# First stage of a hybrid decoder step: the first pair of sequences compressed one at a time, and GpSimd asking for the loads that are not pages

## The chip, the cores and the metric

The kernel runs on one core of a Trainium2 chip. The metric is device time in microseconds (us) for one execution; the median of several runs is given, and the profile is of one more execution. Engines are called as in the profile: PE (TensorE), PEld (its weight loads), DVE (VectorE), ACT (ScalarE), POOL (GpSimd) and SP (SyncE). SPq, ACTq and POOLq are the instruction streams of SP, ACT and POOL in so far as they issue DMAs. All arithmetic inputs and outputs are float32.

## The reference, cut to what matters

One inference step of a one-layer decoder: 512 prompt tokens and 8 sequences of 8 new tokens each, width 1024. Each of the 8 sequences has 2048 past tokens in a paged cache of 128-token pages, 16 pages each, found through `page_table`. The part that the change touches is the compression of the raw keys and values of the past (`compress_blocks`), the norm and the adaLN modulation ahead of the input projection:

```python
def compress_blocks(x, pos, w1, w2):          # x: (sequence, 2048 tokens, 2 groups, 64)
    xc = x.reshape(b, 128, 16, 2, 64)          # chunks of 16 tokens
    lead  = einsum('bncgd,cdh->bngh', xc + pos[0], w1[0])
    trail = einsum('bncgd,cdh->bngh', xc + pos[1], w1[1])
    return einsum('bngh,hd->bngd', silu(lead[:, :-1] + trail[:, 1:]), w2)
# kc = rms_norm(compress_blocks(k_raw, ...)), vc = compress_blocks(v_raw, ...)
mod = silu(c) @ w_ada + b_ada                  # shift, scale, gate
h = rms_norm(x, norm1_g) * (1 + sc1) + sh1
z = h @ w_in                                   # then attention, mixing and the MLP
```

## The kernel before, in words

The first stage (`first_stage`) compresses the past of the 8 sequences, and beside it norms and turns x and computes the first eight pieces of the modulation. The projection `z`, attention and the MLP follow it.

**Units.** The stage is a row of 32 units. Unit `u` works on a pair of sequences `i = u // 8`, on one of four groups of taps `j = (u // 2) % 4`, and on keys or values `kv = u % 2`. For each, DVE copies the page tile `cpg` of each sequence into order (`cmp_order`, tile `ro`, one for two units), PE turns it (`rows_turn`, PSUM tile `ct`, four transposes for each sequence), ACT rounds it into `xh` and DVE takes the rest into `xl` (`split`), in a ring of two buffers. Then PE makes twelve products `hid` over the 512 columns of the pair (`cmp_hidden`). High and low parts of values and weights are kept apart so that three fast products stand for one exact one. In the first eight units the weights of the taps are split in the same way (`cmp_taps`, tiles `w1hlk`, `w1hlv` from `w1rawk`, `w1rawv`).

**Order.** PE's matmuls of this stage are chained in the order of the program text: the turns of unit `u + 1` stand ahead of the products of unit `u`. What else is to be done is hung behind units in the list `todo`: the silu of c (`ada_silu`), the turned constants, the bias of the compression (`posb`), the norm of an x tile (`norm`: a Square on ACT, a short chain on DVE) and its turn one unit later (`nt`), the sums of `w_ada` pieces (`ada`), and the ends of each pair (`cmp_act`, `cmp_out`, `cmp_keys`). For ACT and DVE a planner orders the instructions by a time line of its own, except where the text puts one behind another (`issue_after`).

**Queues.** `dma` puts each transfer behind the previous one of the same engine, so SP's list is in the order of the text. It holds the page table, nearly all pages (each an instruction of 128 KB, its number read from the table into a register; eight numbers are read at once), the x tiles, c, the small constants, `w2` and the `w_ada` pieces. ACT's list holds the first tap weights, eight pages of sequence 1, and the other tap weights. GpSimd issues only two gathers here. The page tile `cpg` has four buffers, the x tile two, and the two raw tap weights share their two buffers (`big`) with the `w_ada` pieces.

Of the kernel before, what the change touches and what calls it, by code (L numbers as in the profile page):

```python
# [45 lines left out]
class Step:  # L46
# [165 lines left out]
    def constants(self):  # L212
        nc, I, c = self.nc, self.I, self.const_tile
        gains = c("gains", [8, P])
        pos = c("pos", [32, P])
        chan = c("chan", [64, P])
        for i, n in enumerate("kv"):
            self.dma("sync", pos[16 * i:16 * i + 16], I[f"cmp_pos_{n}"].rearrange("o (j c) d -> (o j) (c d)", c=2))
        self.dma("sync", c("ptT", [P, 1], I32), I["page_table"].rearrange("b (n o) -> (b n) o", o=1))
        self.dma("sync", chan[0:48], I["b_ada"].rearrange("o (j p) -> (o j) p", p=P))  # L220
        self.dma("sync", chan[48:56], I["norm1_g"].rearrange("o (j p) -> (o j) p", p=P))
        self.dma("sync", chan[56:64], I["norm2_g"].rearrange("o (j p) -> (o j) p", p=P))
        for i, n in enumerate(["fox_qn_g", "nsa_qn_g", "nsa_kn_cmp_g"]):
            self.dma("sync", gains[i:i + 1].rearrange("o (a d) -> o a d", a=2),
                                dram(I[n], 0, [[64, 1], [0, 2], [1, 64]]))
# [13 lines left out]
    def late_constants(self):  # L239
# [13 lines left out]
        kgain = c("kgain", [P, 3, 64])  # L253
        for i, n in enumerate(["fox_kn_g", "nsa_kn_slc_g", "nsa_kn_win_g"]):
            self.dma("sync", kgain[:, i, :], dram(I[n], 0, [[0, P], [1, 64]]))
        self.dma("sync", c("bfox", [P, 8]), dram(I["b_fox_f"], 0, [[0, P], [1, 8]]))
        ts(c("identB", [P, P], BF16), jp, 0.0, None, OP.is_equal)
        ts(c("diagB", [P, P], BF16), jp, 0.0, NEG, OP.is_gt, OP.mult)
        ts(c("triU", [P, P]), jp, 0.0, None, OP.is_ge)


    def ada_start(self):
# [3 lines left out]
        self.dma("sync", c9[0:1], self.I["c_prompt"].rearrange("o (k c) -> o k c", k=NK))  # L266
        self.dma("sync", c9[1:9], self.I["c_sample"].rearrange("b (k c) -> b k c", k=NK))
        self.c9 = c9, c9t
# [17 lines left out]
    def ada_load(self, ch, w):  # L286
        self.dma("sync", w, self.I["w_ada"][0, :, 256 * ch:256 * ch + 256].rearrange("(k p) e -> p k e", p=P))
# [63 lines left out]
    def cmp_weights(self, pl):  # L351
# [7 lines left out]
        for i in range(2):  # L359
            x = [pl.tile([P, 2, 514], F32R, name=f"x{n}{i}") for n in "hl"]  # L360
            for t in x:
                self.nc.vector.memset(t[:, :, 512:514].bitcast(F32), 0.0)
            self.ring.append(x)

    def cmp_taps(self, u):

        taps = lambda w: w.rearrange("p (a j) h -> p a j h", a=4)[:, :, u // 2]
        w = self.w1[u % 2]
        self.split(taps(w[:, 0]), taps(w[:, 1]), taps(self.w1raw[u % 2]))

    def cmp_second(self):

        self.w2 = []
        for n in "kv":
            w2 = self.keep.tile([P, 64], F32, name=f"w2{n}")
            w2r = self.keep.tile([P, 64], F32, name=f"w2raw{n}")
            self.dma("sync", w2r, self.I[f"cmp_w2_{n}"][0])
            self.ts(w2, w2r, 0.5, None, OP.mult)
            self.w2.append(w2)
# [57 lines left out]
    def cmp_order(self, pl, n):  # L437

        self.ros[n] = []
        for b in (2 * (n // 4), 2 * (n // 4) + 1):  # L440
            o = pl.tile([P, 2, 4, 2, 64], F32, tag="ro", bufs=3, name=f"ro{n}_{b}")
            self.cp(o.rearrange("p h x c d -> p h c x d"),
                    self.cpg[b][:, :, 2 * (n % 4):2 * (n % 4) + 2].rearrange("p h c (x d) -> p h c x d", x=4))
            self.ros[n].append(o)

    def rows_turn(self, u):


        n, kv = u // 2, u % 2
        xh, xl = self.ring[u % 2]  # L450
        for s in range(2):
            tb = self.trb(f"ct{u}{s}")
            for g in range(2):
                for h in range(2):
                    self.tr(tb[:, 256 * g + P * h:256 * g + P * h + P],
                            self.ros[n][s][:, h, 2 * kv + g].rearrange("p c d -> p (c d)"))
# [5 lines left out]
    def cmp_hidden(self, u):  # L462
        i, j, kv = u // 8, (u // 2) % 4, u % 2
        if u % 8 == 0:
# [34 lines left out]
    def first_stage(self, pl, pe, hf):  # L499
# [21 lines left out]
        def late():  # L521
            with self.tc.issue_after(self.splits[-1]):
                self.late_constants()
# [20 lines left out]
        todo = {u: [] for u in range(32)}  # L544
        todo[4] += [self.ada_silu]
        todo[5] += [self.constants_turned, self.ada_turned, lambda: ends.update(b=self.cmp_bias(pe)),
                    lambda: self.ada_first_load(pe, 4), lambda: self.ada_first_load(pe, 0)]
        todo[6] += [lambda: self.cmp_bias_end(ends["b"])]
        todo[8] += [late]
# [3 lines left out]
        for b, u in ((4, 4), (5, 6), (6, 12), (7, 14)):  # L553
            todo[u] += [load_x] * (b < 6) + [lambda b=b: self.cmp_tile(pe, b), lambda b=b: self.cmp_pages("sync", b)]
        todo[10] += [load_x]
        for k, u in enumerate((9, 11, 17, 19, 21, 23, 25, 27)):
            todo[u] += [lambda k=k: ends.update({k: self.ada_first(pe, ada[k])})]
            todo[u + 1] += [lambda k=k: ends[k]()]
            if k > 1:
                todo[(12, 14, 18, 20, 22, 24)[k - 2]] += [lambda k=k: self.ada_first_load(pe, ada[k])]  # L560
            if k % 2:
                todo[max(u + 2, 17)] += [lambda k=k: self.modulate(0, hf, range(k - 1, k + 1))]
        self.lfg = {}
        for y, u in enumerate((15, 18)):
            todo[u] += [lambda y=y: self.stage_logf(pe, y)]
            todo[u + 2] += [lambda y=y: self.store_logf(y)]
        for i in range(3):
            for kv in range(2):
                todo[8 * i + 6 + kv] += [lambda i=i, kv=kv: self.cmp_act(pl, i, kv)]
        for i in range(3):  # L570
            for kv in range(2):
                todo[8 * i + 10 + kv] += [lambda i=i, kv=kv: self.cmp_out(pl, i, kv)]
            todo[8 * i + 13] += [lambda i=i: self.cmp_keys(i)]
# [3 lines left out]
        for u in range(32):  # L577
            if u % 2 == 0 and u // 2 + 1 < 16:
                self.cmp_order(pl, u // 2 + 1)
            if u + 1 < 8:  # L580
                self.cmp_taps(u + 1)
            if u + 1 < 32:
                self.rows_turn(u + 1)
            self.cmp_hidden(u)
# [1561 lines left out]
```

## Time and profile before

| | |
|---|---|
| runs | 1265.33, 1269.34, 1272.30 us; median 1269.34 us |
| profiled execution | 1271.95 us, span 1270.1 us |
| busy in the span | PE 1196.8, PEld 1022.9, DVE 695.5, ACT 509.3, POOL 108.9 us |
| matmul clock granted, mean | 0.985 |
| first transposes of pages on PE | at 26.71 us |
| first compression products on PE | at 35.66 us |
| last compression products on PE | end at about 190 us |

In the lines of the timeline a row reads: start in us, time in us, engine, line of the kernel, operation, output and inputs with shapes, count, and in brackets the engine's idle time before it with what ended it. In the chain of waits a row is start, length, and what held the chain. Rows that group instructions give count, busy us, mean ns, and idle time before them. A busy time sums neighbouring, pipelined instructions into their union. In the rows of DMA issues the last number is the median us from issue to landing.

### The profile page before, as it was taken

The page shows a single profiled execution, that of the slowest core. Times are in us where ns is not written, and L with a number is a line of the kernel's source. Part 1 is how long each engine was busy: PE and PEld are TensorE (multiplying, and loading weights), DVE is VectorE, ACT ScalarE, POOL GpSimd, SP SyncE. Part 2 cuts the span into 40 slices and gives each one's busy share as a digit, 9 for nine tenths or more (in the row PEclk, how much of TensorE's full clock was granted, in tenths as well). Part 3 has the DMA queues.
Part 4 walks back from the last instruction along what each step waited for, and adds up shares of the span by engine and source line. Part 5 has one row for each costly group of instructions (what it writes and reads, how often), then busy time and mean ns, then how long its engine had stood idle before and what let it go on. Part 6 is the DMA issues. An engine that isn't in the chain of part 4 may idle for free.

```text
span 1270.1 us, 24582 instructions
## 1 busy us (share of the span) xinstructions
PE 1196.8 (94%) x9379; PEld 1022.9 (81%) x9379; DVE 695.5 (55%) x1888; ACT 509.3 (40%) x1135; POOL 108.9 (9%) x107
## 2 busy tenths in 40 slices
PE   0799999999999999999999998989999999999998
PEld 0677778999666656666799998988989899898896
DVE  2577775676688846555543444666234433333545
ACT  2344444443776854544432323353414123232230
POOL 0000000000221120000200000001011111020110
PEclk9999999999999999999999999998999999999999
DMA  9576518697685359797663233124213223142202
GB/s 205 163 227 188 174 57 271 192 331 230 192 280 177 108 198 302 257 297 245 154 171 92 76 92 100 51 67 133 67 67 100 82 86 100 34 133 67 67 18 75
DMA packets 177067, 188.09 MB, mean 148 GB/s; under 512 B 16901, under 2 KB 158766, under 8 KB 174774
## 3 DMA queue, kind: packets, MB, share of 16 engines
q1 hardware_dynamic: 168134, 178.13, 45.7%
q0 software_dynamic: 3504, 5.24, 1.6%
q10 hardware_dynamic: 5312, 3.15, 1.1%
q8 instruction: 74, 1.21, 0.4%
q14 instruction: 43, 0.35, 0.1%
HBM read 176.48 MB, written 30.90 MB: 163 GB/s over the span
## 4 chain that ended last, share of the span: by engine, by line
PE 84%; DVE 5%; SPq 4%; DMA 4%; ACT 2%; issue 1%; DVEq 0%; ACTq 0%
PE up L77 16%; PE dn L77 16%; PE z L77 8%; PE mg L77 8%; PE wo L77 4%; PE br L77 4%; PE hid L77 4%; PE ss L77 4%; SPq L155 4%; PE k L83 2%; PE so L77 2%; DMA cpg<-in_cache_nsa_kv 2%; PE sp L83 1%; PE ada L77 1%; PE ct L83 1%
## 5 line engine op out<-in xcount | busy, mean ns | idle before, releaser
L77 PE MATMUL z<-winh,h 128*128 128x264 f32 (+1 forms) x576 | 112.2, 287 | 2.4 <-DVE h L723 1.7
L77 PEld LDWEIGHTS z<-winh,h 128*128 128x128 f32 x576 | 92.0, 190 | 5.4 <-DVE h L723 4.2
L1935 POOL TENSOR_TENSOR u<-u 128x576 f32<-128x576 f32 x32 | 53.0, 1659 | 426.8 <-ACT u L112 337.6
L77 PE MATMUL z<-winl,h 128*128 128x264 f32 (+1 forms) x320 | 88.0, 284 | 0.0
L100 DVE TENSOR_TENSOR acc<-acc,dn 128x512 f32<-128x512 f32 x60 | 39.8, 686 | 74.5 <-PE dn L77 74.4
L77 PE MATMUL mg<-hH,wmh 128*128 128x288 f32 x256 | 75.9, 298 | 1.1 <-ACT wmh L112 1.1
L77 PE MATMUL mg<-hH,wml 128*128 128x288 f32 x256 | 75.6, 297 | 0.9 <-DVE wml L131 0.9
L77 PE MATMUL mg<-hL,wmh 128*128 128x288 f32 x256 | 72.7, 295 | 0.0
L83 PE MATMUL ct<-identF,ro 128*128 128x128 f32 x256 | 36.6, 289 | 36.4 <-DVE ro L115 30.3
L112 ACT ACTIVATE xh<-ct 128x256 fp32r<-128x256 f32 x128 | 47.5, 385 | 57.0 <-PE ct L83 35.8
L83 PEld LDWEIGHTS ct<-identF,ro 128*128 128x128 f32 x256 | 30.6, 149 | 40.7 <-DVE ro L115 30.7
L723 DVE TENSOR_TENSOR u<-u,u 128x512 fp32r<-128x512 f32 x64 | 28.3, 484 | 60.8 <-ACT u L112 60.8
L77 PEld LDWEIGHTS z<-winl,h 128*128 128x128 f32 x320 | 60.6, 190 | 0.0
L131 DVE TENSOR_TENSOR xl<-ct,xh 128x256 fp32r<-128x256 f32 x128 | 50.2, 419 | 13.0 <-ACT xh L112 10.2
L131 DVE TENSOR_TENSOR wml<-wmr,wmh 128x1024 fp32r<-128x1024 f32 x16 | 19.6, 1225 | 63.8 <-ACT wmh L112 63.8
L77 PEld LDWEIGHTS mg<-hH,wmh 128*128 128x128 f32 x256 | 48.5, 189 | 1.5 <-ACT wmh L112 1.3
L77 PEld LDWEIGHTS mg<-hH,wml 128*128 128x128 f32 x256 | 48.6, 190 | 1.1 <-DVE wml L131 1.1
L112 ACT ACTIVATE u<-up 128x256 f32<-128x256 f32 (+1 forms) x96 | 27.8, 326 | 52.1 <-PE up L77 51.1
L77 PEld LDWEIGHTS mg<-hL,wmh 128*128 128x128 f32 x256 | 47.1, 188 | 0.1
L77 PE MATMUL hid<-xh,w1hlk 128*128 128x512 f32 x128 | 43.3, 420 | 0.0
L77 PE MATMUL hid<-xh,w1hlv 128*128 128x512 f32 x128 | 41.7, 407 | 0.0
L112 ACT ACTIVATE u<-u 128x576 fp32r<-128x576 f32 x32 | 21.9, 686 | 41.8 <-POOL u L1935 41.8
(928 smaller groups left out, 3553.1 us busy)
## 6 DMA issues: line engine op xcount, KB each, us to landing
adw<-in_w_ada SPq DMA_DIRECT2D x16, 1024.0 KB
foxD<-in_cache_fox_kv SPq DMA_DIRECT2D x128, 128.0 KB
wur<-in_w_up SPq DMA_DIRECT2D x32, 512.0 KB
wdr<-in_w_down SPq DMA_DIRECT2D x32, 512.0 KB
cpg<-in_cache_nsa_kv SPq DMA_DIRECT2D x120, 128.0 KB
fr<-foxD SPq DMA_DIRECT2D x28, 512.0 KB
sr<-in_cache_nsa_kv SPq DMA_DIRECT2D x112, 128.0 KB
wada<-in_w_ada SPq DMA_DIRECT2D x8, 1024.0 KB
```

The costliest lines, as they stand in the source:

```text
L77: ins = self.nc.tensor.matmul(out, a, b, start=start, stop=stop, skip_group_check=True)
L83: ins = self.nc.tensor.transpose(out, in_, self.identF[:n, :n])
L100: self.nc.vector.tensor_tensor(out, a, b, op=op)
L112: return self.nc.scalar.activation(out, in_, f, **kw)
L131: self.splits.append((eng or self.nc.vector).tensor_tensor(l, x, h.bitcast(F32), op=OP.subtract).ins)
L155: self.issued[eng] = getattr(self.nc, eng).dma_start(out, in_).ins
L723: (eng or self.nc.vector).tensor_tensor(h2[:, o:o + n], x[:, i:i + n], h2[:, i:i + n].bitcast(F32), op=OP.subtract)
L1935: nc.gpsimd.tensor_tensor(u[j], u[j], u[j], op=OP.mult)
```

## The change

The 32 units become 40. The first pair's two sequences are done one after the other in eight units each, on 256 columns (`units` lists for each unit its pair, its sequences, `j` and `kv`); the other three pairs keep their eight units of 512 columns. The ring's zero columns are set behind each half. The taps are split in the first eight units as before, now pinned behind the previous unit's last `xh` and `xl`, as are the `ro` copies up to unit 15 and each that begins a new sequence or pair.

SP's list in this stage is left with the page table and pages: eight of sequence 0, all of 1, 2, 3, and later 4 to 7 (and the two stores of gathered log forget values, as before). ACT's eight pages are the second half of sequence 0. All else is issued by GpSimd, in the order of its use: c and the small constants at the start, two x tiles when `xl` of the units 4 and 6 is there (a one-element copy on GpSimd makes it wait), `w2`, the page table's second form, the key gains and the forget bias behind unit 10, then x tiles and `w_ada` pieces in turn. A Tanh of one column is run on ACT ahead of its pages. The constants that DVE computes stand at the start, not behind unit 8; the halving of `w2` is done in place behind unit 18. What hangs behind units is moved on by eight (by eight to ten for some).

The diff, cut:

```diff
@@ constants, late_constants, ada_start @@
-            self.dma("sync", pos[16 * i:16 * i + 16], ...)
-        self.dma("sync", c("ptT", [P, 1], I32), ...)
-        self.dma("sync", chan[0:48], ...)
+            self.dma("gpsimd", pos[16 * i:16 * i + 16], ...)
+        self.dma("gpsimd", chan[0:48], ...)
...
+    def late_loads(self):
+        self.dma("gpsimd", c("ptT", [P, 1], I32), ...)
+        kgain = c("kgain", [P, 3, 64])
+        for i, n in enumerate(["fox_kn_g", "nsa_kn_slc_g", "nsa_kn_win_g"]):
+            self.dma("gpsimd", kgain[:, i, :], ...)
+        self.dma("gpsimd", c("bfox", [P, 8]), ...)
...
-        self.dma("sync", c9[0:1], self.I["c_prompt"]...)
-        self.dma("sync", c9[1:9], self.I["c_sample"]...)
+        self.dma("gpsimd", c9[0:1], self.I["c_prompt"]...)
+        self.dma("gpsimd", c9[1:9], self.I["c_sample"]...)
@@ ada_first_load @@
-        self.ada_load(ch, w)
+        self.ada_load(ch, w, "gpsimd")
@@ cmp_order, rows_turn @@
+        _, bs, j, _ = self.units[u]
+        for b in bs:
+            o = pl.tile([P, 2, 4, 2, 64], F32, tag="ro", bufs=3, name=f"ro{b}_{j}")
...
-        for s in range(2):
+        for b in bs:
+            s = b % 2
             tb = self.trb(f"ct{u}{s}")
@@ cmp_hidden @@
+        c0, w = 256 * (bs[0] % 2), 256 * len(bs)
-            for w, x in three((wh, wl), self.ring[u % 2]):
-                self.mm(self.hid[i][kv], w[:, 4 * a + j, :], x[:, a % 2, a // 2:a // 2 + 512], n == 0, n == 47)
+            for y, x in three((wh, wl), self.ring[u % 2]):
+                self.mm(self.hid[i][kv][:, c0:c0 + w], y[:, 4 * a + j, :], x[:, a % 2, c0 + a // 2:c0 + a // 2 + w],
+                        n == 0, n == 47)
@@ first_stage @@
-            self.dma("sync", xs[k][:TILES[k][1]], self.x_rows(k))
+            self.dma("gpsimd", xs[k][:TILES[k][1]], self.x_rows(k))
+        def behind():
+            both = ExitStack()
+            for i in (self.last_high, self.splits[-1]):
+                both.enter_context(self.tc.issue_after(i))
+            return both
+        self.units = [(b // 2, bs, j, kv) for b, bs in ((0, (0,)), (1, (1,)), (2, (2, 3)), (4, (4, 5)), (6, (6, 7)))
+                      for j in range(4) for kv in range(2)]
-        self.cmp_pages("sync", 0)
-        self.cmp_pages("scalar", 1, slice(0, 8))
+        warm = self.small.tile([P, 1], F32, tag="warm", bufs=1, name="warm")
+        nc.vector.memset(warm, 0.0)
+        self.act(warm, warm, AF.Tanh)
+        self.cmp_pages("sync", 0, slice(0, 8))
+        self.cmp_pages("scalar", 0, slice(8, 16))
         self.cmp_raw(pe, 1)
-        self.cmp_pages("sync", 1, slice(8, 16))
+        self.cmp_pages("sync", 1)
         self.cmp_weights(pl)
-        self.cmp_pages("sync", 2)
-        load_x()
-        self.cmp_pages("sync", 3, slice(0, 8))
-        load_x()
         self.ada_start()
         self.constants()
-        self.cmp_pages("sync", 3, slice(8, 16))
-        self.cmp_second()
+        self.late_constants()
+        self.cmp_pages("sync", 2)
+        self.cmp_pages("sync", 3)
-        todo[4] += [self.ada_silu]
+        todo[9] += [pinned(self.ada_silu)]
+        todo[10] += [self.cmp_second, self.late_loads]
+        todo[18] += [pinned(self.cmp_second_half)]
-        for k, u in enumerate((4, 6, 9, 11, 15)):
-            todo[u - 1] += [lambda k=k: norm(k)]
+        for k, u in enumerate((12, 14, 17, 19, 23)):
+            todo[u - 2] += [lambda k=k: norm(k)]
             todo[u] += [lambda k=k: turned(k)]
+        def asked():
+            x = self.ring[0][1]
+            g = nc.gpsimd.tensor_copy(warm, x[:, 0, 0:1].bitcast(F32))
+            with self.tc.issue_after(g.ins):
+                load_x()
+        todo[3] += [asked]
+        todo[5] += [asked]
+        todo[8] += [pages(4)]
+        todo[12] += [load_x]
+        todo[13] += [wada(0)]
+        todo[14] += [pages(5), load_x]
+        todo[15] += [wada(1)]
+        todo[18] += [load_x]
+        todo[20] += [pages(6)]
+        todo[22] += [pages(7)]
-        for k, u in enumerate((9, 11, 17, 19, 21, 23, 25, 27)):
+        for k, u in enumerate((17, 19, 25, 27, 29, 31, 33, 35)):
...
-                todo[(12, 14, 18, 20, 22, 24)[k - 2]] += [lambda k=k: self.ada_first_load(pe, ada[k])]
+                todo[(20, 22, 26, 28, 30, 32)[k - 2]] += [wada(k)]
...
-        for u in range(32):
-            if u % 2 == 0 and u // 2 + 1 < 16:
-                self.cmp_order(pl, u // 2 + 1)
+        for u in range(40):
+            if u % 2 == 0 and u + 2 < 40 and (u + 2) % 8:
+                with behind() if u + 2 < 16 else nullcontext():
+                    self.cmp_order(pl, u + 2)
             if u + 1 < 8:
-                self.cmp_taps(u + 1)
+                with behind():
+                    self.cmp_taps(u + 1)
             self.rows_turn(u + 1)
+            if (u + 2) % 8 == 0 and u + 2 < 40:
+                with behind():
+                    self.cmp_order(pl, u + 2)
             self.cmp_hidden(u)
```

More of the change, by code (lines that the diff above doesn't have):

```diff
@@ L361, in cmp_weights @@
             for t in x:
-                self.nc.vector.memset(t[:, :, 512:514].bitcast(F32), 0.0)
+                for c in (256, 512):
+                    self.nc.vector.memset(t[:, :, c:c + 2].bitcast(F32), 0.0)
             self.ring.append(x)
     def cmp_taps(self, u):
-        taps = lambda w: w.rearrange("p (a j) h -> p a j h", a=4)[:, :, u // 2]
-        w = self.w1[u % 2]
-        self.split(taps(w[:, 0]), taps(w[:, 1]), taps(self.w1raw[u % 2]))
+        _, _, j, kv = self.units[u]
+        taps = lambda w: w.rearrange("p (a j) h -> p a j h", a=4)[:, :, j]
+        w = self.w1[kv]
+        self.split(taps(w[:, 0]), taps(w[:, 1]), taps(self.w1raw[kv]))
     def cmp_second(self):
@@ L519, in turned, with pinned, g @@
                 self.copy(hf[:, 4 * h:4 * h + 4, t0:t0 + m], self.norm_turned(xs[k], 0, k, h))
-        def late():
-            with self.tc.issue_after(self.splits[-1]):
-                self.late_constants()
+        def behind():
[3 more added lines that the diff above has]
+            return both
+        def pinned(f):
+            def g():
+                with behind():
+                    f()
+            return g
+        self.units = [(b // 2, bs, j, kv) for b, bs in ((0, (0,)), (1, (1,)), (2, (2, 3)), (4, (4, 5)), (6, (6, 7)))
+                      for j in range(4) for kv in range(2)]
         self.page_rows()
@@ L548, in first_stage @@
-        todo[6] += [lambda: self.cmp_bias_end(ends["b"])]
-        todo[8] += [late]
-        for k, u in enumerate((4, 6, 9, 11, 15)):
-            todo[u - 1] += [lambda k=k: norm(k)]
-            todo[u] += [lambda k=k: turned(k)]
-        for b, u in ((4, 4), (5, 6), (6, 12), (7, 14)):
-            todo[u] += [load_x] * (b < 6) + [lambda b=b: self.cmp_tile(pe, b), lambda b=b: self.cmp_pages("sync", b)]
-        todo[10] += [load_x]
-        for k, u in enumerate((9, 11, 17, 19, 21, 23, 25, 27)):
+        todo = {u: [] for u in range(40)}
```

75 lines of the change are left out of this document (37 added, 38 removed).

## The prediction

> **What bounds the kernel now.** I read the page first, then busy time by stretch, the chain of waits, and the timelines of the queues and engines. On the page, the chain that ended last:
>
> ```profile
> PE 84%; DVE 5%; SPq 4%; DMA 4%; ACT 2%; issue 1%; DVEq 0%; ACTq 0%
> ```
>
> TensorE sets the end; SP's list and DMA hold 8%, some 100 us. Busy times by stretch (length, then PE, PEld, DVE, ACT, POOL, clock, DMA share, GB/s) say where the rest lies:
>
> ```profile
> 26.70:35.60 8.90, 3.77 (x16) 3.00 (x17) 4.90 (x10) 2.20 (x6) 0.00 (x0) 1.00 0.56 162
> 35.60:50.60 15.00, 15.00 (x73) 12.49 (x73) 6.63 (x15) 4.46 (x12) 0.00 (x0) 1.00 0.70 208
> 50.60:78.60 28.00, 22.11 (x176) 18.29 (x175) 18.08 (x64) 12.17 (x28) 1.21 (x1) 0.94 0.49 144
> 78.60:190.00 111.40, 107.78 (x696) 85.72 (x694) 82.94 (x282) 52.99 (x128) 0.98 (x1) 1.00 0.55 160
> ```
>
> PE begins at 26.7. At 78.6 the eighth unit of the first pair has passed its `hid` products. From there to 190, the rest of the first stage, PE idles 3.6 of 111.4 us. So after 78.6 the stage is PE's own work, and whatever brings 78.6 forward should bring the end forward. Before it PE is idle for 26.7 + 5.1 + 5.9 us. The timelines show on what (PE, then ACT, then SP's list):
>
> ```profile
> 26.71 1.12 PE L83 MATMUL ct<-identF,ro 128*128 128x128 f32 x4 [26.71 <-DVE ro L115]
> ...
> 35.66 1.20 PE L77 MATMUL hid<-xh,w1hlk 128*128 128x512 f32 x2
> ...
> 39.84 1.04 PE L83 MATMUL ct<-identF,ro 128*128 128x128 f32 x8
> ...
> 55.56 1.90 PE L83 MATMUL ct<-identF,ro 128*128 128x128 f32 x8 [4.54 <-DVE xl L131]
> 57.11 1.20 PE L77 MATMUL hid<-xh,w1hlk 128*128 128x512 f32 x2
> ```
> ```profile
> 12.80 1.62 ACTq L155 DMA_DIRECT2D w1rawv<-in_cmp_w_v  x2
> 14.45 1.28 ACT L112 ACT_TABLE_LOAD   x1 [14.45 <-DMA cpg<-in_cache_nsa_kv]
> 15.75 2.19 ACT L112 ACTIVATE w1hlk<-w1rawk 128x512 fp32r<-128x512 f32 x4
> 22.72 2.19 ACT L112 ACTIVATE w1hlv<-w1rawv 128x512 fp32r<-128x512 f32 x4 [4.79 <-DMA w1rawv<-in_cmp_w_v]
> ...
> 52.66 1.05 ACT L112 ACTIVATE adw<-adw 9x1024 f32<-9x1024 f32 x1 [3.77 <-DMA adw<-in_c_sample]
> ```
> ```profile
> 2.92 38.10 SPq L155 DMA_DIRECT2D cpg<-in_cache_nsa_kv  x40
> ...
> 49.56 0.76 SPq L155 DMA_DIRECT2D adw<-in_c_sample  x1
> ```
>
> Two things stand out. The first `hid` waits until 35.66, because a unit needs the pages of both sequences. And at 48.9 ACT, which works in order, stands on the Tanh over c_sample, whose load SP asks for only at 49.56, behind page after page; `xh` stands behind it, PE idles 4.5 us, and starts again slowly (the eight `ct` at 55.56 take 1.90, those at 39.84 1.04).
>
> **The change, part by part.** *When the first half-width units can run.* The order of bytes hardly changes until 14 us: SP still sends eight pages of sequence 0 first, and ACT's eight pages are now the other half of the same sequence instead of half of sequence 1. ACT's queue goes in order, and behind those pages come the two halves of w1rawv, which the split at 22.72 finds landed. So ACT's pages have landed by 22.7 at the latest, SP's first eight well before: sequence 0 is ready at 17 to 22 us, and the first `ct` follows one copy later, against 26.7 now. But the second unit needs the v taps: w1rawv at 22.7, plus the table load that the new warm Tanh puts ahead of ACT's pages, 1.28 us, partly under the wait for the page table (0.4 taken, bounds 0 and 1.28), plus one tap on ACT (2.19/4) and one on DVE, then `xh` and `xl`. Its `hid` starts at 25.0 (bounds 23.5 and 28).
>
> *PE's work from there to the end of the first pair.* From the chain of waits and the groups by shape:
>
> ```profile
> 139.48 2.79 PE hid L77 x12
> ...
> 142.49 0.87 PE ct L83 x8
> ...
> 211.52 12.96 PE z L77 x107
> ```
> ```profile
> L131 DVE TENSOR_TENSOR xl<-ct,xh 128x256 fp32r<-128x256 f32 x128 | 50.2, 419 | 13.0 <-ACT xh L112 10.2
> L131 DVE TENSOR_TENSOR w1hlv<-w1rawv,w1hlv 128x512 fp32r<-128x512 f32 x4 | 2.6, 686 | 4.5 <-ACT w1hlv L112 4.5
> L115 DVE COPY ro<-cpg 128x1024 f32<-128x1024 f32 x32 | 21.1, 690 | 14.6 <-PE ct L83 11.3 <-DMA cpg<-in_cache_nsa_kv 3.1
> ```
>
> A pair's unit costs PE 2.79 + 0.87 = 3.66 us. Half as wide, twelve `hid` products of 256 columns cost 12 × 0.121 (the pace of the 264-wide `z`) = 1.45, and four `ct` 0.44: 1.89 us. Their sum over 16 units is 30.2 against 29.3, so the doubled weight loads cost about 1 us; I use 1.89. After the first unit and the second's `ct`, 30.2 - 1.89 - 0.44 = 27.9 is left. Other work between 50.6 and 78.6 (bias, two x tiles turned): 22.11 - 4 × 3.66 = 7.5, of which the slow restart is about 1.8 (those `ct` hold PE 1.55 until `hid` begins instead of 0.87, and the first two `hid` behind them take 1.20 as at 35.66, where twelve lost 1.4 in all; I take 1.1); 5.7 is left, and the restart goes with the stall, c_sample being asked for in the first microseconds. The cold beginning stays: 4.2 us from 35.66 to 39.84 for one `hid`, 1.4 over the warm 2.79. Idle time is what I know least: the old stretch had 1.35 beside the stall, and half units leave less cover, since two `xh` and two `xl` after a `ct` take about as long as the 1.89 us that PE has meanwhile. I take 5. Sum: 25.0 + 27.9 + 5.7 + 1.4 + 5 = 65.0.
>
> *DVE's work in the same stretch.* 4.90 + 6.63 + 18.08 = 29.6 us, plus seven taps, which used to be done before PE began and now stand pinned between the units: 7 × 0.69 = 4.8. Together 34.4. The most that DVE was busy in a ten-microsecond stretch of the first stage is this:
>
> ```profile
> 80.00:90.00 10.00, 8.07 (x55) 5.88 (x53) 8.34 (x45) 4.32 (x11) 0.00 (x0) 1.00 1.07 323
> ```
>
> At that share, 34.4/0.834 = 41.2, so 66.2. PE's and DVE's ends fall together, and where two bounds are level the result is a little behind both: I take 67.3, 11.3 us before 78.6.
>
> *Pages for the next pair.* Sequences 2 and 3 must be there some 4 us before that. The new list of SP has 24 pages to the end of sequence 1, as the old one had to the middle of sequence 1; these rows of the chain give the next group and its pitch, and a landing:
>
> ```profile
> 28.33 0.53 SPq L162
> ...
> 34.71 0.52 SPq L162
> ...
> 79.89 9.09 DMA x<-in_x_prompt
> ...
> 108.16 2.58 DMA cpg<-in_cache_nsa_kv
> ```
>
> Four groups of eight at 6.4 us end at 53.9, landed at 56.5: no wait. If the two x tiles (1 MB), now in a queue beside, slow SP's pages to the 162 GB/s of 26.7:35.6, it is some 63, level with the need. What comes off SP's list hides nothing after that: the remaining pages have more lead than before.
>
> *Loads by GpSimd.* Its engine is idle all through this stage, and its own rows late in the kernel give the price:
>
> ```profile
> hH<-hfd POOLq DMA_DIRECT2D x1, 2304.0 KB, 13.1
> hL<-hfd POOLq DMA_DIRECT2D x8, 256.0 KB, 4.9
> ```
>
> Interpolated, a 512 KB x tile lands in about 6 us, 1 MB of w_ada in 8. The tight one is the third x: asked for at unit 12, squared on ACT after unit 15, three half units and two turned tiles later, about 8 us. In order behind that Square stand ACT's `xh`, then DVE and PE. At the 9.1 us of the x row above it costs 1 to 2 us; on the other side the constants now run while DVE is idle at the start, and the halving of w2 no longer stands ahead of `xl`. I let the two cancel (bounds -2 and +3). The w_ada loads have two or more full units of lead. GpSimd's new one-element copies wait for `xl`; behind them stand only its own loads, and the `xl` two units later waits for a copy that is long done: 0. The added memsets and the moved constants lie before the first page. After 190 nothing is edited; I shift it whole.
>
> The Trainium skill speaks against this part: "SBUF — State Buffer", section "SBUF: two separate sides", says that a DMA asked for by GpSimd cannot get its descriptors written while a VectorE copy in a two-port mode holds the shared port, and gives 620 ns growing to 3100. No row here shows it. By it each of the three tightly timed x tiles would land up to 2.5 us later, the sum would lose up to 7.5, and the gain would be about 4.
>
> *Sum.* The profiled execution took 1271.95 us with a span of 1270.1 and 1.85 around it; the median of the runs, 1269.34, lies 2.6 lower. 1271.95 - 11.3 = 1260.6 against the profile, 1258.0 as a median. With idle 1.35 and full speed the pair ends near 62 (gain 16); with idle 9, near 71.5 (gain 7): 1253 to 1262.
>
> **The rivals.** *DVE becomes the bound (18%).* For it: 34.4 us of DVE work, now in strict order with the units; its share in 50.6:78.6 is 0.65, in 78.6:190 0.745. Against it: PE, not DVE, set the pace there. At 0.745 the pair ends at 71.2, at 0.65 at 78: gain 7.4 to 0.6, 1262 to 1269.
>
> *GpSimd's loads come late (12%), slower.* Each x holds one of two buffers, so x tiles three, four and five follow one another in one in-order queue with w_ada between, and each late microsecond holds ACT, then PE. The forecast's 11.3 is used up when the five x and first w_ada loads together come 11.3 us late; it is slower by over 0.5% from 17.7 late. With x landing at 14 instead of 8 us three times, and a slow restart of 1.8 each, 23 us are lost: 1281. For it: the load row of 9.1 us. Against it: GpSimd's landings of 4.9 and 13.1 us, on calmer DMA. The rule of the port would push this way, yet not this far.
>
> *The clock stays low (8%), slower.* After an idle stretch PE runs at about half speed: 1.20 for two `hid` and 1.90 for eight `ct`. If the gaps between half units never let it warm, each costs up to 1.89 us more, sixteen some 29 over the 1.4 counted, less the 5 of idle time that this fills: 1282 if all are cold, 1270 if half. It decides from about ten units. Against it: at the old start one group of twelve was enough (the `ct` at 39.84 are quick), and a PE that is slow has no gaps. The Trainium skill, "TensorE: Matmul & The Clock Gate", section "Part 1: The HAM clock gate", has it cool only after an idle window of about 3.4 us; the trace agrees in so far as the 4.54 us at 55.56 did it. By that rule gaps of well under a microsecond leave it warm.
>
> *The change doesn't do what it says (2%)*: the planner lets another wait stand where c_sample's stood; 1269.
>
> **How the numbers follow.** A measurement tells 0.5%, 6.3 us, from no change: below 1263 is faster. Forecast 60%, all faster. DVE 18%, half faster, half the same. Loads 12% and clock 8%, slower. Nothing done 2%, the same. So 0.69, 0.11, 0.20. The range for 8 in 10 runs from 1252 to 1275: the forecast, DVE's rival and the nearer part of the slow ones; the forecast's own is 1253 to 1262.
>
> **What would show it.** In the new profile: the first `hid` near 21 and the second unit's near 25 us; no ACT wait on c_sample, and no PE gap over 3 us before the second pair; the second pair's first `hid` near 67; DVE at 0.75 to 0.85 busy between; the stage's last `hid` near 178 instead of 190. I am wrong if ACT's Squares wait on x, if DVE waits for pages of sequence 2 or 3, or if half-width products stay at 0.21 us for more than the first two units.

## The result, and the profile after

The changed kernel takes 1261.37 us (median of 7 runs, 1257.43 to 1264.78) beside 1270.24 us of the kernel before (7 runs on the same chip): ratio 0.9933, 95% interval 0.9914 to 0.9952. It is faster by 8.9 us, as forecast in sign, inside the range, and 3.4 us above the forecast's 1258.0. The profiled execution took 1260.9 us with a span of 1259.1.

The chain that ended last, from the page:

```profile
PE 83%; DVE 6%; DMA 4%; ACT 2%; SPq 2%; issue 1%; DVEq 0%; ACTq 0%
```

SP's share is halved. Busy times by stretch (length, PE, PEld, DVE, ACT, POOL, clock, DMA share, GB/s), cut where the new kernel's stretches end (a packet's time counts in the stretch in which it starts, so a DMA share can pass 1):

```profile
18.30:23.90 5.60, 5.46 (x24) 5.13 (x25) 3.42 (x9) 2.58 (x6) 0.00 (x0) 1.00 1.15 244
23.90:57.70 33.80, 31.70 (x307) 29.97 (x306) 24.53 (x74) 16.62 (x40) 6.90 (x13) 1.00 0.79 209
57.70:68.70 11.00, 5.99 (x28) 5.99 (x29) 5.94 (x13) 4.35 (x9) 1.45 (x2) 0.69 0.99 276
68.70:178.00 109.30, 107.87 (x697) 85.85 (x695) 82.68 (x266) 51.97 (x127) 8.08 (x10) 1.00 0.54 155
```

Up to 57.7 PE is idle for only 2.2 us (1.48 of them in one gap). Then come eleven microseconds in which it works for six, at a granted clock of 0.69. The end of the first pair's products, which stood at 78.6, is now at 68.7. The rest of the stage takes 109.3 instead of 111.4 us. PE's timeline, from the first transposes on:

```profile
18.36 1.97 PE L83 MATMUL ct<-identF,ro 128*128 128x128 f32 x8 [18.36 <-DVE ro L115]
19.98 0.78 PE L77 MATMUL hid<-xh,w1hlk 128*128 128x256 f32 x2
...
23.95 0.96 PE L77 MATMUL hid<-xh,w1hlv 128*128 128x256 f32 x2
...
38.02 0.63 PE L83 MATMUL ct<-identF,ro 128*128 128x128 f32 x4 [1.48 <-DVE ro L115]
...
57.35 0.28 PE L77 MATMUL hid<-xl,w1hlk 128*128 128x256 f32 x1
62.72 1.97 PE L83 MATMUL nt<-identF,x 128*128 128x128 f32 x8 [5.08 <-DVE x L104]
64.48 1.92 PE L83 MATMUL ct<-identF,ro 128*128 128x128 f32 x8
66.04 0.78 PE L77 MATMUL hid<-xh,w1hlv 128*128 128x256 f32 x2
...
177.46 0.39 PE L77 MATMUL hid<-xl,w1hlv 128*128 128x512 f32 x1
```

The 4.54 us behind c_sample are gone, and 5.08 us stand ahead of the second pair instead. PE waits there for `x`, an x tile that DVE has normalized. DVE's timeline, the chain of waits and GpSimd's timeline show why that is late:

```profile
60.03 1.29 DVE L115 COPY ro<-cpg 128x1024 f32<-128x1024 f32 x2 [1.32 <-DMA cpg<-in_cache_nsa_kv]
61.24 0.15 DVE L109 SCALAR_TENSOR_TENSOR nrs<-ntt,nrs 128x1 f32<-128x1 f32 x1
61.31 0.69 DVE L109 SCALAR_TENSOR_TENSOR cst<-cst,csx 128x512 f32<-128x512 f32 x1
61.91 0.75 DVE L104 TENSOR_SCALAR x<-x,nrs 128x1024 f32<-128x1024 f32 x1
```
```profile
53.90 0.54 SPq L155
...
54.62 5.03 DMA cpg<-in_cache_nsa_kv
...
66.39 2.55 PE hid L77 x12
```
```profile
54.19 0.54 POOL L155 DMA_DIRECT2D x<-in_x_prompt  x1 [16.20 <-DMA cpg<-in_cache_nsa_kv]
54.80 0.91 POOL L155 DMA_DIRECT2D wada<-in_w_ada  x1
```

SP issues the last page of sequence 3 at 54.6, one page in 0.72 us, and it lands 5.03 us later, at 59.65. DVE's copy of sequence 3's rows, which waits for it, stands in DVE's order ahead of the end of the normalization. So the wait for pages holds the normalization, that holds PE's turn of x (`nt`), and behind that in PE's order stand the `ct` of the second pair and the first pair's last products. GpSimd asked for a third x tile and the first `w_ada` piece, 1.5 MB together, in the same microseconds as the last pages.

### The profile page after: what moved, and what is told of

The parts are those of the page before. It is cut to its first block, busy times and chain, and to the rows that moved or that the text cites. A ratio compares the mean times of both kernels' runs of the same rounds, so it can differ in the third digit from the quotient of the medians.

```text
span 1259.1 us, 24790 instructions
## 1 busy us (share of the span) xinstructions
PE 1200.7 (95%) x9475; PEld 1030.0 (82%) x9475; DVE 695.4 (55%) x1893; ACT 509.4 (40%) x1136; POOL 130.3 (10%) x139
## 4 chain that ended last, share of the span: by engine, by line
PE 83%; DVE 6%; DMA 4%; ACT 2%; SPq 2%; issue 1%; DVEq 0%; ACTq 0%
PE dn L77 17%; PE up L77 16%; PE z L77 9%; PE mg L77 8%; PE hid L77 5%; PE br L77 4%; PE ss L77 4%; PE wo L77 3%; SPq L155 2%; PE k L83 2%; DMA cpg<-in_cache_nsa_kv 2%; PE so L77 2%; PE ct L83 2%; PE ada L77 2%; PE sp L83 1%
## 5 line engine op out<-in xcount | busy, mean ns | idle before, releaser
L77 PE MATMUL hid<-xh,w1hlv 128*128 128x512 f32 (+1 forms) x160 | 45.2, 369 | 0.5 <-ACT xh L112 0.4
L77 PE MATMUL hid<-xh,w1hlk 128*128 128x512 f32 (+1 forms) x160 | 45.0, 369 | 0.1
```

The source lines that it names most:

```text
L77: ins = self.nc.tensor.matmul(out, a, b, start=start, stop=stop, skip_group_check=True)
```

## The experiments

Every ratio is to the kernel before, run on the same chip. The copy's start is given for the runs that keep the changed kernel's units and queues.

| run | median, us | ratio (95%) | first copy of sequence 3's rows starts | last `hid` of the stage starts |
|---|---|---|---|---|
| changed kernel | 1261.37 | 0.9933 (0.9914 to 0.9952) | 60.03 | 177.46 |
| c_only | 1269.65 | 1.0011 (1.0000 to 1.0022) | | 190.09 |
| all_sp | 1282.49 | 1.0108 (1.0091 to 1.0125) | | 194.43 |
| pair_newq | 1267.25 | 0.9993 (0.9983 to 1.0004) | | 186.56 |
| again (unchanged) | 1257.88 | 0.9918 (0.9896 to 0.9941) | 64.27 | 181.32 |
| f_wada | 1256.98 | 0.9927 (0.9904 to 0.9950) | 60.50 | 177.01 |
| f_norm | 1259.42 | 0.9937 (0.9921 to 0.9954) | 64.96 | 177.79 |
| f_ro8 | 1262.32 | 0.9957 (0.9943 to 0.9971) | 63.23 | 180.12 |
| f_all | 1257.41 | 0.9919 (0.9902 to 0.9936) | 60.32 | 173.79 |
| g_act | 1264.24 | 0.9972 (0.9960 to 0.9983) | waits for no page | 179.65 |
| g_best | 1258.80 | 0.9930 (0.9912 to 0.9948) | waits for no page | 174.60 |
| again2 (unchanged) | 1261.91 | 0.9955 (0.9937 to 0.9972) | 60.93 | 178.34 |
| f_all2 (as f_all) | 1257.30 | 0.9914 (0.9897 to 0.9932) | 59.72 | 172.78 |

**c_only: the stall on c_sample taken away alone.** In the kernel before:

```diff
-        self.dma("sync", c9[0:1], self.I["c_prompt"]...)
-        self.dma("sync", c9[1:9], self.I["c_sample"]...)
+        self.dma("gpsimd", c9[0:1], self.I["c_prompt"]...)
+        self.dma("gpsimd", c9[1:9], self.I["c_sample"]...)
```

> The kernel before, with nothing changed but the two loads of c, which GpSimd asks for at the start. Theory 1 (both halves of the change count: the removed stall on c_sample, and the earlier start by half-width units): the 4.5 us gap at 50.6 and the slow restart go, the rest of the start stays as it was; the last hid of the stage ends near 184 instead of 190, 1264 to 1266 us against 1270. Rival (the gain is the c_sample stall alone, the half units give nothing): the last hid ends near 178 as in the changed kernel, about 1261 us. Second rival (something stands right behind the stall, such as x or the pages of sequence 3): less than 2 us gained.

It gained nothing. DVE's and PE's timelines:

```profile
52.85 0.15 DVE L106 TENSOR_SCALAR lfrow<-ptT 128x1 int32<-128x1 int32 x1 [3.48 <-DMA ptT<-in_page_table]
```
```profile
54.31 1.11 PE L83 MATMUL ct<-identF,ro 128*128 128x128 f32 x8 [2.67 <-DVE xl L131]
60.42 1.09 PE L83 MATMUL nt<-identF,x 128*128 128x128 f32 x8 [2.22 <-DVE x L104]
```

ACT no longer waits for c_sample, but DVE now stands for 3.48 us on the page table's second form, another small load in SP's list. PE's one gap of 4.54 us became two of 2.67 and 2.22. A stall behind a mixed in-order list had the next stall right behind it.

**all_sp: one sequence at a time, but all loads of this stage on SP's list again,** at the same places of the text.

```diff
...
-            self.dma("gpsimd", xs[k][:TILES[k][1]], self.x_rows(k))
+            self.dma("sync", xs[k][:TILES[k][1]], self.x_rows(k))
...
-            x = self.ring[0][1]
-            g = nc.gpsimd.tensor_copy(warm, x[:, 0, 0:1].bitcast(F32))
-            with self.tc.issue_after(g.ins):
-                load_x()
+            load_x()
```

> The changed kernel with every load that GpSimd was given put back on SP, at the same place in the order of the text (pages of sequences 0 and 1, then c and the small constants, then pages of 2 and 3, then x tiles, w2, key gains and w_ada in turn, without the one-element copies). Theory 1 (GpSimd's list saves SP's issue time, some 11 issues of 0.4 to 0.8 us ahead of the pages of sequence 2): pages of sequence 3 land some 5 us later than now, about 65 us, and the second pair waits by as much; x tiles stand behind the pages in SP's list, so the first Square comes at 62 or later and the turn of x stands in PE's chain ahead of unit 13: a stall of 5 to 15 us; 1266 to 1276 us. Rival (x and w_ada by GpSimd collide with the last pages, so that the old queue is as good): 1259 to 1263 us.

Slower than the kernel before, and by more than expected. The timelines of SP, ACT and PE:

```profile
60.40 1.05 SPq L155 DMA_DIRECT2D x<-in_x_prompt  x2
```
```profile
64.37 1.06 ACT L112 ACTIVATE sq<-x 128x1024 bf16<-128x1024 f32 x1 [12.78 <-DMA x<-in_x_prompt]
```
```profile
69.88 1.94 PE L83 MATMUL nt<-identF,x 128*128 128x128 f32 x8 [18.00 <-DVE ntt L100]
```

SP comes to x only behind all pages of sequences 0 to 3. PE began at 17.5 and then stood for 18 us: the early start was given back whole, and more. This is not the kernel before with half units, though: there SP asked for the first x at 41.07, ahead of the pages of sequence 3, and here at 60.40, behind them. Half units with x at its old place in SP's list were not run.

**pair_newq: the new queues, but the first pair as eight units of 512 columns.**

```diff
-        self.units = [... for b, bs in ((0, (0,)), (1, (1,)), (2, (2, 3)), (4, (4, 5)), (6, (6, 7)))
+        self.units = [... for b, bs in ((0, (0, 1)), (2, (2, 3)), (4, (4, 5)), (6, (6, 7)))
```

> The changed kernel with all its queues, but the first pair compressed as one again: 8 units of 512 columns in place of 16 of 256, the rest of the list hung behind the unit that does the same share. Theory 1: the first hid waits for both sequences as before (near 35 us), no c_sample stall; PE then has more cover for each unit; the last hid of the stage near 183 to 185; 1264 to 1266 us. Rival (the half units give nothing): the last hid near 178, 1261 us. If DVE was the bound of the half units, this one makes up part of its later start and ends within 2 us of the changed kernel.

Also no gain. PE's timeline:

```profile
31.82 1.97 PE L83 MATMUL ct<-identF,ro 128*128 128x128 f32 x8 [12.42 <-DVE ro L115]
...
74.47 1.97 PE L83 MATMUL nt<-identF,x 128*128 128x128 f32 x8 [4.17 <-DVE nti L106]
```

The first unit waits for the pages of sequence 1 until 31.8. The stage ends 2.9 us earlier than before; the kernel, within the interval, at the same time. So the new queues without half units are worth nothing, half units cost 1.1% in the one order of SP's list that was run, and both together gain 0.7%: moving the loads only pays if there is work to do early, and the early units gain nothing when a load that they meet on the way stands behind the pages. Whether a better order of SP's list would have done as well as GpSimd is open.

**again, again2: the changed kernel repeated,** to see how far the new wait varies.

> The changed kernel once more, unchanged. Ratio 0.991 to 0.995. Theory 1: the first stage ends 12 us earlier again to within 0.5 us, and what the total shows more or less than that lies after it, in the pace of the MLP's products, which in the two profiles so far was 392 and 396 ns for one dn product without any edit there. Rival (the changed kernel loses something of its own later on): the MLP is slow by the same 3 us again.

> The changed kernel once more, on the same chip as the next one, to tell how far the wait for the pages of sequence 3 varies: if that wait is set by when GpSimd's 512 KB of x and 1 MB of w_ada meet the last pages, TensorE's idle time before the second pair is again 5 to 10 us, and the ratio to the kernel before 0.991 to 0.994.

It varies. In again, with the same instructions (DVE, then PE):

```profile
64.27 1.29 DVE L115 COPY ro<-cpg 128x1024 f32<-128x1024 f32 x2 [5.44 <-DMA cpg<-in_cache_nsa_kv]
```
```profile
66.95 1.97 PE L83 MATMUL nt<-identF,x 128*128 128x128 f32 x8 [9.20 <-DVE x L104]
```

The pages are there 4.2 us later than in the first profile, and the stage ends 3.9 us later. In again2 PE's gap is 5.61 us.

**f_wada, f_norm, f_ro8: three small edits to the changed kernel, each alone.**

```diff
@@ f_wada @@
-        todo[13] += [wada(0)]
-        todo[15] += [wada(1)]
+        todo[16] += [wada(0)]
+        todo[17] += [wada(1)]
@@ f_norm: the row copy of unit 16 also behind the last scale of the normalization @@
-                with behind():
+                with behind(), self.tc.issue_after(self.normed_x) if u + 2 == 16 else nullcontext():
...
-        self.ts(sq[:m], x[:m], rs[:m], None, OP.mult)
+        self.normed_x = self.nc.vector.tensor_scalar(sq[:m], x[:m], rs[:m], None, op0=OP.mult).ins
@@ f_ro8: the row copy of unit 8 at the ordinary place @@
-            if u % 2 == 0 and u + 2 < 40 and (u + 2) % 8:
+            if u % 2 == 0 and u + 2 < 40 and ((u + 2) % 8 or u + 2 == 8):
-            if (u + 2) % 8 == 0 and u + 2 < 40:
+            if (u + 2) % 8 == 0 and 8 < u + 2 < 40:
```

> The changed kernel with the first two w_ada loads asked for three and two units later (todo 16 and 17 instead of 13 and 15), so that GpSimd's 1 MB no longer shares the DMA engines with the last pages of sequences 2 and 3. Theory 1 (the 5.1 us, in another run 9.2 us, in which TensorE idles before the second pair come from the landing of those pages, and that is late because GpSimd's w_ada stands beside them): the last page lands 2 to 3 us earlier, near 57, the idle time falls to about 2 to 3 us, the stage's last hid ends 2 to 3 us earlier (near 175 to 176) and the total is 1.5 to 3 us below the changed kernel's. Theory 2 (the pages are bound by SP's own list, 0.72 us each, and the loss is DVE's order): nothing moves, total within 1 us of the changed kernel's.

> The changed kernel with the copy of sequences 2 and 3's rows (ro) put behind the end of the second x tile's normalization in VectorE's order, instead of ahead of it. Theory 2 (the cost is VectorE's order: the copy that waits for pages has the normalization queued behind it, and with it TensorE's turn of x, which stands ahead of the pair's first products): nt comes 2 to 3 us earlier, the idle time splits or falls below 3 us, TensorE restarts warm, and the stage ends 2 to 3 us earlier, as does the total. Theory 1 (the landing alone decides): the idle time moves from ahead of nt to behind it, ct starts at the same time or 1 to 2 us earlier, total 0 to 1.5 us less.

> The changed kernel with the row copy of sequence 1's first step at its ordinary place, one unit earlier, instead of behind the turn of the unit before. The 1.48 us in which TensorE waits for ro at 38.02 goes. If TensorE's sum sets the end of the first pair: total 1 to 1.5 us less. If the wait for the pages of sequences 2 and 3 sets it: the 1.5 us come back as a longer wait there, total within 0.5 us of the changed kernel's.

*f_wada* did not do what its theory said. PE's gap was 5.85 us and the stage ended as in the first profile. Busy times by stretch, first of the changed kernel, then of f_wada, show that the traffic did go:

```profile
60.00:65.00 5.00, 2.29 (x11) 2.29 (x12) 2.91 (x6) 0.60 (x1) 0.02 (x1) 0.70 1.08 281
```
```profile
60.00:65.00 5.00, 1.82 (x9) 1.82 (x10) 2.63 (x5) 0.60 (x1) 0.00 (x0) 0.54 0.51 148
```

Why it changed nothing, the times of the requests suggest. The eight profiles of the changed kernel and its small edits, in the order of the last column:

| profile | GpSimd asks for the third x tile | for the first `w_ada` | SP asks for the last page of sequence 3 | its copy starts | later by |
|---|---|---|---|---|---|
| f_all | 51.89 | 58.82 | 56.16 | 60.32 | 4.2 |
| f_all2 | 52.03 | 58.95 | 55.54 | 59.72 | 4.2 |
| changed kernel | 54.19 | 54.80 | 54.62 | 60.03 | 5.4 |
| f_wada | 53.89 | 66.06 | 54.56 | 60.50 | 5.9 |
| again2 | 54.56 | 55.18 | 54.69 | 60.93 | 6.2 |
| f_ro8 | 52.42 | 53.03 | 54.97 | 63.23 | 8.3 |
| again | 54.31 | 54.92 | 55.64 | 64.27 | 8.6 |
| f_norm | 54.24 | 54.85 | 55.84 | 64.96 | 9.1 |

Where the last page is asked for ahead of the `w_ada` piece, the copy starts 4.2 to 6.2 us later; where it is asked for behind it, 8.3 to 9.1. In the changed kernel's first profile the page was ahead by 0.18 us, so by this reading f_wada had nothing to gain against it. All eight profiles fit, and the three with `w_ada` moved back stay in the lower group; that the piece delays the page is the simplest reading, but no run fixed the order of the two requests by itself. The lower group still lies above the 2.6 us of a calm landing, and there the third x tile had been asked for ahead of the page; no run moved that tile alone, so its share is argued only.

*f_norm* is the clearest. PE, then DVE:

```profile
59.16 1.09 PE L83 MATMUL nt<-identF,x 128*128 128x128 f32 x8 [1.49 <-DVE x L691]
...
65.80 1.09 PE L83 MATMUL ct<-identF,ro 128*128 128x128 f32 x4 [5.11 <-DVE ro L115]
```
```profile
64.96 1.29 DVE L115 COPY ro<-cpg 128x1024 f32<-128x1024 f32 x2 [5.25 <-DMA cpg<-in_cache_nsa_kv]
```

The turn of x no longer waits for pages, and the idle time moves behind it, as the landing theory had it. From the start of the copy to sequence 3's first `ct` it is 0.84 us now, 5.3 before (60.03 to 65.33, the fifth of the eight `ct` at 64.48). The first table says what that is worth: from the copy's start to the last `hid` it is 112.8 to 113.5 us in the three profiles with the new order (f_norm, f_all, f_all2) and 116.5 to 117.4 in the five with the old one. So DVE's order, with the slow restart behind it, cost about 4 us, and the landing the rest. In this execution the pages came at 65.0 and ate the gain; the ratio over all runs, 0.9937, shows none either.

*f_ro8*: the gap of 1.48 us is gone, and PE waits 10.07 us before the second pair. The saved time came back as a longer wait, as its second branch said, and 3.5 us more with it, since in this execution the pages came at 63.2.

**f_all, f_all2: the three edits together.**

> All three edits together. If theory 1 and 2 both hold in part, TensorE's idle time before the second pair falls below 2 us and it restarts warm: 4 to 6 us below the changed kernel's, some 1252 to 1254. If the pages' own list is the bound, no more than 1 to 2 us below it.

> The changed kernel with all three small edits (w_ada later, the row copy behind the normalization, sequence 1's first row copy earlier) beside the unedited one. If its 4 to 8 us earlier end of the stage reach the end of the kernel: 2 to 5 us below the changed kernel run beside it, ratio 0.988 to 0.991. If later stages take them back: within 1.5 us of it.

PE's timeline of f_all2:

```profile
56.95 1.09 PE L83 MATMUL nt<-identF,x 128*128 128x128 f32 x8 [1.48 <-DVE x L691]
...
60.56 0.63 PE L83 MATMUL ct<-identF,ro 128*128 128x128 f32 x4 [2.08 <-DVE ro L115]
```

The last `hid` starts at 172.78, 4.7 to 8.5 us earlier than in the three profiles of the changed kernel. Side by side with the changed kernel it takes 1257.30 against 1261.91 us, ratios 0.9914 (0.9897 to 0.9932) and 0.9955 (0.9937 to 0.9972). Over all runs the two are nearer, since the changed kernel's other ratios are 0.9918 and 0.9933, inside the reach of this version's: a further gain is likely, not shown. The 1252 to 1254 us hoped for of f_all did not come; there PE still waited 1.49 and 2.94 us, and the clock fell again (0.50 in 64:66).

**g_act, g_best: SP's list made shorter.** SP needs 0.72 us for a page, and before the last page of sequence 3 it has 55 others; its list, not the DMA engines, could be what holds the copy's start near 60 even in the good profiles. Two stretches of the changed kernel speak for it (DMA share 0.59 and 0.60):

```profile
45.00:50.00 5.00, 5.00 (x93) 4.47 (x93) 4.13 (x21) 2.19 (x5) 0.00 (x0) 1.00 0.59 185
50.00:55.00 5.00, 5.00 (x45) 4.88 (x43) 4.05 (x14) 2.96 (x7) 0.73 (x2) 1.00 0.60 165
```

So ACT was given the last eight pages of sequence 3, one behind each of the units 2 to 9:

```diff
-        self.cmp_pages("sync", 3)
+        self.cmp_pages("sync", 3, slice(0, 8))
...
+        for k in range(8):
+            todo[k + 2] += [pinned(lambda k=k: acted(k))]
```

> The changed kernel with the last eight pages of sequence 3 asked for by ScalarE, one in each of units 2 to 9 of the first pair, instead of by SP as the last of its list. Theory 3 (SP's list is the bound between the first and the second pair: 56 pages at 0.72 us each, with 6.7 to 8.2 us of waits of SP's own queue, bring the last issue to 54.6 to 57.5 us, while the DMA engines are busy only 0.5 to 0.6 of the time between 45 and 55 us): the last page lands before 57, the copy of the rows waits for no page, TensorE's idle time before the second pair falls from 5 to 10 us to under 2.5 us without a cold restart, the stage's last hid starts at 170 to 173 instead of 177 to 181, and the total is 4 to 8 us below the changed kernel's (ratio about 0.987). Rival (the DMA engines or GpSimd's x and w_ada loads bound the landing, or ScalarE's 0.55 to 0.72 us for each page delays its high halves): idle time of the same size, or the same time lost in gaps of 0.7 us inside the first pair; total within 2 us of the changed kernel's.

> The same eight pages by ScalarE and the three earlier edits (w_ada two units later, the row copy behind the normalization, sequence 1's first row copy one unit earlier). If theory 3 holds, 1 to 3 us below the kernel with ScalarE's pages alone, some 1250 to 1253, the stage's last hid at 168 to 171; if not, as the three edits alone, 1257.

The theory was right on the landing and wrong on the time. No copy waits for a page any more. But ACT's and PE's timelines have this:

```profile
44.16 0.38 ACT L112 ACTIVATE xh<-ct 128x256 fp32r<-128x256 f32 x1 [4.30 <-DMA cpg<-in_cache_nsa_kv]
```
```profile
44.59 0.68 PE L77 MATMUL hid<-xh,w1hlv 128*128 128x256 f32 x2 [2.55 <-ACT xh L112]
...
65.41 1.97 PE L83 MATMUL nt<-identF,x 128*128 128x128 f32 x8 [3.69 <-DVE x L104]
```

ACT's own page instruction at 43.56 had to wait for an earlier page to land (the chain of waits puts that page's request at 35.42, on SP, and its landing 8.13 us later), and `xh` stood behind it for 4.30 us. PE lost 2.55 us, restarted slowly, and came to the second pair later; there DVE, busy 4.59 of the 5 us from 60 to 65, was behind with the normalization. With the three edits (g_best) the stage ends as in f_all, with the idle time elsewhere. So shortening SP's list in this way moved the wait from SP's queue into ACT's and gained nothing.

## Why the prediction was right, and which steps of it were not

**The gain.** Against the profiles, 1260.6 was forecast and 1260.9 measured; the forecast median of 1258.0 missed because it kept the kernel before's distance of 2.6 us between profile and median, while the changed kernel's profile lay 0.5 us below its median. The size is right in part by errors that cancel.

**The first units: right.** First `hid` at 19.98 (near 21), the second unit's at 23.95 (25.0), products at full pace within the second unit. The rival of a clock that stays low did not come.

**PE's sum: idle term mis-sized.** 5 us of idle time were taken; 2.2 came. The 1.4 us of the cold beginning were added behind the second unit's start, though most of them lie in the first unit: the second unit's products took 2.0 us (23.95 to 25.95) where the third's took 1.5, so only 0.5 belonged there. Half units do cover their own chain. What the last unit takes at full pace stands in the chain of waits of again, before its stall:

```profile
53.14 0.87 PE nt L83 x8
...
54.45 1.43 PE hid L77 x12
```

Without the wait for pages the first pair would have ended near 60.8 (57.63, where its products stop, then 0.87 for the turn of x, 0.87 for eight `ct` and 1.43 for twelve products, 3.17 together), against the sum's 65.0. The earlier start (1.05 us) and the two terms make up the difference to within 0.7 us.

**DVE level with PE: wrong as a bound, right as an amount.** Its work from 18.3 to 68.7 is 33.9 us (34.4 forecast). But it was busy 0.71 of the time up to 57.7 while PE idled 2.2, so DVE did not set the end; that rival did not come either. (The share of 0.834 was not quite the highest of the old stage either: 115:125 has 8.54 us in ten.)

**Pages "no wait": the step that failed.** SP's pitch was right (last issue forecast at 53.9, measured 54.62). The landing was not: 2.6 us were taken from a calm row, 5.03 came, and in again the copy started 8.6 us after the last page was asked for. The forecast weighed two x tiles beside these pages, and not the third and the first `w_ada` piece, which GpSimd asked for at 54.19 and 54.80. It also set the need some 4 us before 67.3, when PE was ready at 57.6. And it did not see that the waiting copy stands in DVE's order ahead of the normalization; the three profiles with the other order put about 4 us on that. Two of the forecast's own signs fired here: a PE gap over 3 us before the second pair, and DVE waiting for pages of sequence 2 or 3.

**"The restart goes with the stall": wrong in sum.** A wait of 5.08 us gave a new slow restart: from 62.72 to 68.94 PE needed 6.2 us for what takes 3.17. The wait and the restart cost 8.1 us and brought 60.8 to 68.9. Two misses of opposite sign, 65.0 against 60.8 and 0 against 8.1, with the 2.3 us put on top of both bounds, left 9.9 of the forecast's 11.3 us at the end of the first pair. That they nearly cancel was luck.

**"I let the two cancel": wrong to the good.** The rest of the stage is 2.1 us shorter (PE idles 1.4 us instead of 3.6). No Square waited for x, which landed in 5.0 us, and `w_ada` in 6.6 (6 and 8 were interpolated):

```profile
x<-in_x_prompt POOLq DMA_DIRECT2D x4, 512.0 KB, 5.0
wada<-in_w_ada POOLq DMA_DIRECT2D x8, 1024.0 KB, 6.6
```

The rule of the Trainium skill that spoke against this part ("SBUF — State Buffer", "SBUF: two separate sides") would have had GpSimd's transfers late beside a VectorE copy in a two-port mode. The trace shows no such lateness, since both medians are below what was interpolated, but it hardly puts the rule to the test: of DVE's row copies only the one at 30.45 meets a request for x (29.95 to 30.51). The rival of late loads did come in one form that was not thought of: not GpSimd's loads late for ACT, but SP's pages late beside them.

**"After 190 nothing is edited, shifted whole": off by 1.0.** The stage's end moved by 12.0 us and the span by 11.0. From the last `hid` to the end it is 1077.5 to 1082.2 us in the profiles of all these kernels. The three with the earliest end of the stage (f_all2, f_all, g_best) stand at 1080.8 to 1081.8, so part of an earlier end may be lost later; this spread stays open.

**What stays open.** The late landings (the copy near 64 in again, near 60 in the first profile) go with the last page being asked for behind the `w_ada` piece; no run fixes that order, and none moves the third x tile alone. Half units with x at its old place in SP's list were not run.

## What to carry to other kernels

An early start is worth what the next wait leaves of it: here the move of the loads gave nothing alone, the split of the first pair lost time with the loads behind the pages, and the two gave 0.7% together. When an edit brings work forward, go through everything that the work meets on the way, transfers issued in the same microseconds by other queues too, and set each need by the new time. An instruction that waits for a transfer should stand last in its engine's order; putting one copy behind a normalization took about 4 us out of the way from the landing to the end of the stage.

## What the runs showed of the hardware that was not expected

In g_act PE's clock fell for a gap of 2.55 us, and fell only after PE had resumed. Busy times by stretch (PE's busy time is the second number, the granted clock the third from the end):

```profile
42.00:44.00 2.00, 0.04 (x1) 0.00 (x0) 0.00 (x0) 0.00 (x0) 0.00 (x0) 1.00 0.72 150
44.00:46.00 2.00, 1.41 (x5) 1.21 (x6) 0.85 (x2) 0.95 (x3) 0.00 (x0) 0.69 0.72 224
46.00:48.00 2.00, 2.00 (x11) 2.00 (x10) 1.31 (x4) 1.51 (x3) 0.00 (x0) 0.50 0.81 222
```

PE worked from 44.59 on, and half of the clock was granted until about 48. The prediction drew on the Trainium skill, "TensorE: Matmul & The Clock Gate", "Part 1: The HAM clock gate", for an idle window of about 3.4 us; here shorter gaps were enough. But the length of a gap alone does not decide: in g_best (first two lines) a gap of 1.91 us was followed by half of the clock, while in c_only the gap of 2.67 us that ends at 54.31 left it at 1.00 (third line), as f_all2's gaps of 1.48 and 2.08 us did.

```profile
42.91 0.79 PE L77 MATMUL hid<-xh,w1hlv 128*128 128x256 f32 x2 [1.91 <-ACT xh L112]
43.00:46.00 3.00, 3.00 (x13) 2.87 (x14) 1.73 (x5) 1.76 (x4) 0.00 (x0) 0.50 0.69 187
54.00:56.00 2.00, 1.69 (x12) 1.52 (x13) 1.26 (x7) 1.89 (x5) 0.36 (x1) 1.00 0.36 107
```

In these traces the granted clock changes only in steps of 3.41 us (half of it for 3.41 us in g_act, 6.83 in the changed kernel, 10.24 in again), so where a gap lies between two steps may count as much as its length; that is argued, not tested. The second thing: a page instruction on ACT can hold ACT's own arithmetic for 4.30 us, until an earlier page has landed.
